# A transformer block with 32 experts on one core: the first norm's factor on columns, two weight streams alternating

## The chip, the core and the metric

The kernel runs on one core of a Trainium2 chip. The core has a matrix engine (PE, with its weight loads shown apart as PEld), a vector engine (DVE), a scalar engine (ACT), a general engine (POOL), a queue that only issues transfers (SP) and 16 DMA engines. The metric is device time in microseconds (us). All data is 32-bit float, and one product of a 128x128 block with 256 columns shows as two weight loads and two matmuls.

## What is computed

One block over 256 tokens of width 1024, batch 1. The part that the change touches is the front: a modulation row from the condition vector, an RMS norm of `x`, and the query projection; a second norm is that of the context `ctx`.

```python
def rms_norm(x, g):
    return x * lax.rsqrt(jnp.mean(x * x, axis=-1, keepdims=True) + RMS_EPS) * g

sh1, sc1, g1, sh2, sc2, g2 = silu(c) @ w_mod + b_mod        # six parts of 1024
csh1, csc1, ...            = silu(c_ctx) @ w_mod + b_mod
h  = rms_norm(x, norm1_g) * (1 + sc1) + sh1
hc = rms_norm(ctx, norm1_g) * (1 + csc1) + csh1
p  = h @ w_in            # keys, values, queries, gates
k_c, v_c = hc @ w_in[:, :512]
# global and windowed attention, gates, output projection, x = x + g1 * (...)
# second norm, router, top 4 of 32 experts, x = x + g2 * moe(...), final norm
```

## The kernel before, in words

Everything is kept transposed at the front: `x` is eight chunks of 128 features (partitions) by 256 tokens (columns), `x[:, k, :]`. So the norm's mean runs over partitions, and its factor differs from column to column.

**Streams.** All weights come on the SP queue in the order of one list, `pieces` (lines 58 to 80). A ring of eight areas, each of two halves of 1 MB, receives them; `pump` issues the next piece as soon as a half (or, for expert weights, a whole area) is free, and `done` gives a half back and calls `pump`. At the start the sixteen halves take the eight blocks `m0` (1 MB each, the modulation's shift and scale for one chunk) and the eight blocks `q` (0.5 MB each, the query weights for one chunk). The list runs `m0` 0, 1, 2, then `q` 0, `m0` 3, `q` 1 and so on: the query's blocks run two behind. `xc` (the context) is between them. ACT issues a few small transfers itself, among them a table of constants (line 296) behind the third query block.

**Norm of x (lines 205 to 218).** Each chunk is squared (five on DVE, three on ACT), and PE multiplies each square by a 128x128 matrix of ones into `ssp`, so that every partition of `ssp` has the column sums. `inv_norm` takes the square root of all 128x256 values on ACT and the reciprocal on DVE into the tile `rinv`. Then each chunk is multiplied by `rinv` (line 266, six on DVE and two on POOL).

**Modulation.** `m0_prod(j)` (line 235) multiplies the condition columns `cmod` by block `m0[j]`, in 16 small instructions; ACT copies the result to `msb`. `m0_turn(j)` (lines 243 to 248) turns it into columns on PE (`mtp`); DVE adds the bias (L244), forms the scale (L246) and modulates chunk `j` in place (L248). `crow_half` (lines 255 and 257) broadcasts `cmod` to rows `crow` on PE and ACT; the remaining modulation (`mod` blocks, on DVE and POOL, from 51 us on) needs `crow`.

**Queries.** For chunk `j`, `q_prods` adds eight products into the two PSUM tiles `qa`. The loop over `j` runs `m0_prod(j + 2)`, half of `q_prods(j)`, `m0_turn(j + 2)`, the other half. `m0` 0 and 1 and both halves of `crow` lie ahead of the loop.

**Context norm (lines 408 to 413).** During the loop ACT and POOL square and sum the context into one 128x512 tile `csq[0]`. After the second gate (`gate(1)`, line 375) PE multiplies it by ones into `csp`, `inv_norm` makes `rinv_c`, and `modulate_c` (lines 284 and 285) scales the context in place. The key projection `kp` (line 365) of `x` comes next on PE, and the context's own later.

The order on each engine is that of the program. PE takes its instructions in that order, and an instruction that waits holds back all behind it.

Of the kernel before, what the change touches and what calls it, by code (L numbers as in the profile page):

```python
# [34 lines left out]
def tile_dit_block(ctx: ExitStack, tc: tile.TileContext, xcT, consts, small, rows,  # L35
# [21 lines left out]

    for j in range(10):
        if j < 8:
            pieces.append(("m0", j, w_m0[j]))  # L60
        if j > 1:
            pieces.append(("q", j - 2, w_q[j - 2]))
        if j == 6:
            pieces.append(("xc", 0, None))
# [127 lines left out]
    th = f1.tile([128, 8, 2], F32, name="th")  # L192
    nc.scalar.activation(out=th, in_=cc, func=AF.Tanh, scale=0.5)
    nc.scalar.activation(out=junk, in_=eps, func=AF.Sqrt)
    cmod = f1.tile([128, 8, 32], F32, name="cmod")
    nc.vector.memset(cmod, 0.0)
    nc.vector.scalar_tensor_tensor(out=th, in0=th, scalar=1.0, in1=cc, op0=ALU.add, op1=ALU.mult)
    nc.vector.tensor_scalar(out=cmod[:, :, 0:2], in0=th, scalar1=0.5, scalar2=None, op0=ALU.mult)


    def t1(name):
        return f1.tile([128, 256], F32, name=name, tag="t1", bufs=5)

    ssp = ps1.tile([128, 512], F32, name="ssp", tag="y")
    for k in range(8):
        sq = t1("sq")
        v = x[:, k, :]
        if k in (0, 1, 2, 5, 7):
            nc.vector.tensor_tensor(out=sq, in0=v, in1=v, op=ALU.mult)
        else:  # L210
            nc.scalar.activation(out=sq, in_=v, func=AF.Square)
        nc.tensor.matmul(ssp[:, 0:256], ones, sq, start=(k == 0), stop=(k == 7))

    def inv_norm(ps):
        r = t1("rinv")
        nc.scalar.activation(out=r, in_=ps, func=AF.Sqrt, bias=eps, scale=1.0 / 1024)
        nc.vector.reciprocal(r, r)
        return r

# [8 lines left out]
    def m0_prod(j):  # L228


        w = take("m0", j).rearrange("p (k c) -> p k c", k=8)
        mp = ps1.tile([128, 512], F32, name="mp", tag="tp", bufs=2)
        for k in range(8):
            g = 32 * (k % 4)
            nc.tensor.matmul(mp[g:g + 32, 0:256], cmod[:, k, :], w[:, k, :], start=(k < 4), stop=(k >= 4))
        done("m0", j)
        msb_t[j] = t1("msb")
        nc.scalar.copy(out=msb_t[j], in_=mp[:, 0:256])
# [12 lines left out]
    def crow_half(h):  # L251
# [5 lines left out]
        nc.scalar.copy(out=crow[:, 512 * h:512 * h + 512], in_=cps)  # L257

    m0_prod(0)
    rinv = inv_norm(ssp[:, 0:256])  # L260
    m0_prod(1)
    crow_half(0)
    crow_half(1)
    for k in range(8):
        v = x[:, k, :]
        (nc.gpsimd if k >= 6 else nc.vector).tensor_tensor(out=v, in0=v, in1=rinv, op=ALU.mult)
        if k in (0, 2):
            m0_turn(k // 2)

# [17 lines left out]
    for j in range(8):  # L287
        if j < 6:
            m0_prod(j + 2)
        q_prods(j, range(4))  # L290
        if j < 6:
            m0_turn(j + 2)
        q_prods(j, range(4, 8))
        done("q", j)
        if j == 2:
            nc.scalar.dma_start(out=cst, in_=consts[:, C_KEEP:C_TRI])
            nc.scalar.dma_start(out=sinkb, in_=rows[0:1, 0:8].to_broadcast([128, 8]))
# [109 lines left out]
    q_chunk(3)  # L407
    csp = ps1.tile([128, 512], F32, name="csp", tag="tp", bufs=2)
    for i in range(2):
        nc.tensor.matmul(csp[:, 0:256], ones, csq[0][:, 256 * i:256 * i + 256], start=(i == 0), stop=(i == 1))  # L410
    rinv_c = inv_norm(csp[:, 0:256])
    nc.scalar.dma_start(out=tmk, in_=consts[:, C_TRI:C_END])
# [797 lines left out]
```

## Time and profile before

| | us |
|---|---|
| median of 3 runs (1194.88 to 1195.83) | 1195.11 |
| the profiled execution | 1195.13 |
| its span, first to last instruction | 1193.4 |
| PE busy in the span | 1142.9 (96%) |
| DVE, ACT, POOL busy | 359.4, 139.5, 35.7 |
| share of PE, DMA, DVE, ACT in the chain that ended last | 57%, 36%, 4%, 2% |

The chain is followed back from the last instruction: each step is what released the one after it, or the instruction ahead of it on its engine. A stretch of the chain that lies on PE with no gap says that PE was the limit there. A group in the timeline merges neighbours: its length is from its first start to its last end. The granted clock is a share of TensorE's 2.4 GHz.

### The profile page before, as it was taken

The page shows a single profiled execution, that of the slowest core. Times are in us where ns is not written, and L with a number is a line of the kernel's source. Part 1 is how long each engine was busy: PE and PEld are TensorE (multiplying, and loading weights), DVE is VectorE, ACT ScalarE, POOL GpSimd, SP SyncE. Part 2 cuts the span into 40 slices and gives each one's busy share as a digit, 9 for nine tenths or more (in the row PEclk, how much of TensorE's full clock was granted, in tenths as well). Part 3 has the DMA queues.
Part 4 walks back from the last instruction along what each step waited for, and adds up shares of the span by engine and source line. Part 5 has one row for each costly group of instructions (what it writes and reads, how often), then busy time and mean ns, then how long its engine had stood idle before and what let it go on. Part 6 is the DMA issues. An engine that isn't in the chain of part 4 may idle for free.

```text
span 1193.4 us, 13447 instructions
## 1 busy us (share of the span) xinstructions
PE 1142.9 (96%) x5722; PEld 539.0 (45%) x5722; DVE 359.4 (30%) x767; ACT 139.5 (12%) x313; POOL 35.7 (3%) x31
## 2 busy tenths in 40 slices
PE   7999999999999999999999999999898989899996
PEld 5888666884434333443434343434232424233334
DVE  3274666332122232222232222222221212121222
ACT  2122554012000000000000000000000000000012
POOL 0232000000000000000000000000000000000001
PEclk9999999999999999999999999999999999999999
DMA  9995634948999999999999999999999999999994
GB/s 378 383 387 211 225 128 153 390 177 351 427 429 426 428 426 428 429 427 428 426 429 426 429 426 428 427 428 428 428 427 427 428 428 426 429 427 429 425 428 181
DMA packets 37952, 458.34 MB, mean 384 GB/s; under 512 B 4600, under 2 KB 4992, under 8 KB 7424
## 3 DMA queue, kind: packets, MB, share of 16 engines
q1 hardware_dynamic: 36144, 454.05, 91.0%
q10 hardware_dynamic: 1744, 3.38, 0.7%
q8 instruction: 47, 0.77, 0.3%
q14 instruction: 17, 0.14, 0.0%
HBM read 456.36 MB, written 1.05 MB: 383 GB/s over the span
## 4 chain that ended last, share of the span: by engine, by line
PE 57%; DMA 36%; DVE 4%; ACT 2%; issue 1%; ACTq 0%; SPq 0%; DVEq 0%
DMA ring<-w 26%; PE u L845 20%; DMA xx<-w 10%; PE y L884 9%; PE mm L375 3%; PE xg L812 3%; PE u L695 3%; PE qa L276 2%; PE o L705 2%; PE sp L901 2%; PE br L579 2%; ACT xx L517 1%; PE yl L985 1%; PE kp L365 1%; PE vp L449 1%; DVE st L507 1%
## 5 line engine op out<-in xcount | busy, mean ns | idle before, releaser
L845 PE MATMUL u<-ring,t 128*64 128x512 f32 x1632 | 373.8, 598 | 16.1 <-DMA ring<-w 15.7
L845 PEld LDWEIGHTS u<-ring,t 128*64 128x64 f32 x1632 | 112.6, 137 | 233.3 <-issue 201.2
L884 PE MATMUL y<-ring,r_q 128*64 128x512 f32 x768 | 168.9, 592 | 0.0
L891 DVE TENSOR_TENSOR t<-y,r_kv 64x512 f32<-64x512 f32 x60 | 41.3, 689 | 325.3 <-PE y L884 324.9
L884 PEld LDWEIGHTS y<-ring,r_q 128*64 128x64 f32 x768 | 55.2, 137 | 109.6 <-issue 107.9
L858 DVE TENSOR_SCALAR r_q<-u 128x512 f32<-128x512 f32 x32 | 22.1, 692 | 248.6 <-PE u L845 248.6
L860 ACT ACTIVATE r_q<-r_q 128x512 f32<-128x512 f32 x32 | 20.1, 629 | 510.0 <-DVE r_q L858 510.0
L695 PE MATMUL u<-mtx,keep 128*64 128x512 f32 x256 | 62.2, 604 | 3.0 <-DVE r_q L861 3.0
L812 PEld LDWEIGHTS xg<-mtx,r_y 128*128 128x128 f32 x512 | 58.4, 192 | 12.2 <-issue 12.2
L812 PE MATMUL xg<-mtx,r_y 128*128 128x128 f32 x512 | 61.3, 278 | 0.0
L375 PE MATMUL mm<-xx,ring 128*128 128x256 f32 x256 | 59.9, 385 | 0.0
L901 PE MATMUL sp<-t,mtx 128*128 128x512 f32 x120 | 59.7, 620 | 0.0
L375 PEld LDWEIGHTS mm<-xx,ring 128*128 128x128 f32 x256 | 47.3, 190 | 12.6 <-issue 5.0
L845 PE MATMUL u<-xx,t 128*64 128x512 f32 x208 | 48.7, 610 | 3.7 <-DMA xx<-w 3.6
L845 PE MATMUL u<-ptt,t 128*64 128x512 f32 x208 | 48.8, 598 | 0.9 <-DMA ptt<-w 0.9
L814 DVE TENSOR_TENSOR t<-xg,modb 128x512 f32<-128x512 f32 x32 | 22.1, 692 | 86.3 <-PE xg L812 86.3
L901 PEld LDWEIGHTS sp<-t,mtx 128*128 128x128 f32 x120 | 20.5, 191 | 39.5 <-issue 39.5
L902 DVE TENSOR_TENSOR r_t<-r_t,sp 128x512 f32<-128x512 f32 x60 | 38.3, 680 | 0.0
L695 PEld LDWEIGHTS u<-mtx,keep 128*64 128x64 f32 x256 | 16.3, 135 | 44.6 <-issue 22.6
L874 ACT COPY r_q<-ta 128x512 f32<-128x512 f32 x32 | 18.8, 586 | 146.6 <-PE ta L871 146.6
L276 PE MATMUL qa<-xx,ring 128*128 128x256 f32 x128 | 30.7, 388 | 0.0
L845 PEld LDWEIGHTS u<-xx,t 128*64 128x64 f32 x208 | 14.7, 139 | 35.3 <-issue 28.1
(229 smaller groups left out, 897.4 us busy)
## 6 DMA issues: line engine op xcount, KB each, us to landing
ring<-w SPq DMA_DIRECT2D x149, 2048.0 KB, 32.4
xx<-w SPq DMA_DIRECT2D x19, 2048.0 KB, 31.0
ptt<-w SPq DMA_DIRECT2D x19, 2048.0 KB, 32.4
ring<-w_mod SPq DMA_DIRECT2D x16, 1024.0 KB, 11.2
ring<-w_in SPq DMA_DIRECT2D x10, 1024.0 KB, 9.1
ring<-w_m SPq DMA_DIRECT2D x8, 1024.0 KB, 12.6
ring<-w2l SPq DMA_DIRECT2D x3, 2048.0 KB, 34.3
ring<-w_q SPq DMA_DIRECT2D x8, 512.0 KB, 12.1
```

The source lines that it names most:

```text
L276: nc.tensor.matmul(qa[c // 4][:, c % 4, :], w[:, 128 * c:128 * c + 128], x[:, j, :], start=(j == 0 and c % 2 == 0), stop=(j == 7), skip_gr ...
L375: nc.tensor.matmul(gp[0][:, 0:256], w[:, k, :], x[:, k, :], start=(k == 0), stop=(k == 7))
L579: nc.tensor.matmul(ps[:, 0:256], w[:, k, 128 * (m % 2):128 * (m % 2) + 128], Y[:, 4 * br + k, :], start=(k == 0), stop=(k == 3))
L695: nc.tensor.matmul(u[c0:c0 + 64, ch % 2, :], ident[:, 4 * e + ch:4 * e + ch + 1].to_broadcast([128, 64]), be1, start=True, stop=False)
L705: nc.tensor.matmul(ps[:, 0:256], w[:, k, :], M[:, k, :], start=(k == 0), stop=(k == 7))
L812: nc.tensor.matmul(xp[:, b, :], z[:, tb, 128 * k:128 * k + 128], S[:, tb, :], start=(tb == 0), stop=(tb == 1))
L814: nc.vector.tensor_tensor(out=XT[p][:, 4 * h:4 * h + 4, :], in0=xp, in1=sh2[:, 4 * h:4 * h + 4].unsqueeze(2).to_broadcast([128, 4, 128]), ...
L845: nc.tensor.matmul(u[c0:c0 + 64, ch % 2, :], XT[p][:, k, 64 * j:64 * j + 64], w[:, 512 * ch:512 * ch + 512], start=False, stop=(k == 7))
L884: nc.tensor.matmul(y[64 * h:64 * h + 64, :], l, w[:, 512 * h:512 * h + 512], start=(k == 0), stop=(k == 7))
L891: nc.vector.tensor_tensor(out=YY[p][64 * j:64 * j + 64, 512 * h:512 * h + 512], in0=y[64 * h:64 * h + 64, :], in1=g2[64 * h:64 * h + 64, 5 ...
L901: nc.tensor.matmul(sp, t[:, tb, :], y[:, s], start=True, stop=True)
L902: nc.vector.tensor_tensor(out=ACC[0][:, tb, s], in0=ACC[0][:, tb, s], in1=sp, op=ALU.add)
```

## The change

It does six things. The list alternates `m0[j]`, `q[j]`, with `xc` after the sixth pair. The squares of `x` are formed two chunks at a time (two passes of 128x512 on DVE, two on ACT) and added up on DVE to one 128x512 tile `sqx[0]`. `inv_norm` takes such a tile: four products of a 128x128 piece of it with one column of ones give the sums with tokens on partitions, ACT and DVE work on 128x2 values, and two products spread the factor over rows, in PSUM. `m0_prod(0)` comes behind it. All eight products with the factor are on DVE. In the loop `m0_prod` and `m0_turn` run one ahead instead of two, and the two halves of `crow` are inside it, after `j` = 2 and 3. The context's norm uses the same `inv_norm`.

```diff
-    for j in range(10):
-        if j < 8:
-            pieces.append(("m0", j, w_m0[j]))
-        if j > 1:
-            pieces.append(("q", j - 2, w_q[j - 2]))
-        if j == 6:
+    for j in range(8):
+        pieces.append(("m0", j, w_m0[j]))
+        pieces.append(("q", j, w_q[j]))
+        if j == 5:
             pieces.append(("xc", 0, None))
...
+    for i in range(2):
+        for j in range(2):
+            v = x[:, 4 * i + 2 * j:4 * i + 2 * j + 2, :].rearrange("p a b -> p (a b)")
+            if j == 0:
+                nc.vector.tensor_tensor(out=sqx[2 * i], in0=v, in1=v, op=ALU.mult)
+            else:
+                nc.scalar.activation(out=sqx[2 * i + 1], in_=v, func=AF.Square)
+        if i == 0:
+            nc.scalar.activation(out=th, in_=cc, func=AF.Tanh, scale=0.5)
+        nc.vector.tensor_tensor(out=sqx[2 * i], in0=sqx[2 * i], in1=sqx[2 * i + 1], op=ALU.add)
+        if i == 0:
+            nc.vector.scalar_tensor_tensor(out=th, in0=th, scalar=1.0, in1=cc, op0=ALU.add, op1=ALU.mult)
+            nc.vector.tensor_scalar(out=cmod[:, :, 0:2], in0=th, scalar1=0.5, scalar2=None, op0=ALU.mult)
+    nc.scalar.activation(out=junk, in_=eps, func=AF.Sqrt)
+    nc.vector.tensor_tensor(out=sqx[0], in0=sqx[0], in1=sqx[2], op=ALU.add)
+
+    def inv_norm(sq, tag, bufs):
+
+        ps = ps1.tile([128, 512], F32, name="ssp", tag=tag, bufs=bufs)
+        for qt in range(2):
+            for i in range(2):
+                nc.tensor.matmul(ps[:, 256 + qt:257 + qt], sq[:, 256 * i + 128 * qt:256 * i + 128 * qt + 128],
+                                 ones[:, 0:1], start=(i == 0), stop=(i == 1))
+        r = f1.tile([128, 2], F32, name="rn", tag="rn", bufs=2)
+        nc.scalar.activation(out=r, in_=ps[:, 256:258], func=AF.Sqrt, bias=eps, scale=1.0 / 1024)
         nc.vector.reciprocal(r, r)
-        return r
+        for qt in range(2):
+            nc.tensor.matmul(ps[:, 128 * qt:128 * qt + 128], r[:, qt:qt + 1].to_broadcast([128, 128]), ident,
+                             start=True, stop=True)
+        return ps[:, 0:256]
...
+    rinv = inv_norm(sqx[0], "y", 1)
     m0_prod(0)
-    rinv = inv_norm(ssp[:, 0:256])
-    m0_prod(1)
-    crow_half(0)
-    crow_half(1)
     for k in range(8):
-        v = x[:, k, :]
-        (nc.gpsimd if k >= 6 else nc.vector).tensor_tensor(out=v, in0=v, in1=rinv, op=ALU.mult)
-        if k in (0, 2):
-            m0_turn(k // 2)
+        nc.vector.tensor_tensor(out=x[:, k, :], in0=x[:, k, :], in1=rinv, op=ALU.mult)
+        if k == 0:
+            m0_turn(0)
...
     for j in range(8):
-        if j < 6:
-            m0_prod(j + 2)
+        if 0 < j < 7:
+            m0_prod(j + 1)
         q_prods(j, range(4))
-        if j < 6:
-            m0_turn(j + 2)
+        if j == 0:
+            m0_prod(1)
+        elif j < 7:
+            m0_turn(j + 1)
         q_prods(j, range(4, 8))
         done("q", j)
+        if j == 0:
+            m0_turn(1)
+        if j in (2, 3):
+            crow_half(j - 2)
...
-    csp = ps1.tile([128, 512], F32, name="csp", tag="tp", bufs=2)
-    for i in range(2):
-        nc.tensor.matmul(csp[:, 0:256], ones, csq[0][:, 256 * i:256 * i + 256], start=(i == 0), stop=(i == 1))
-    rinv_c = inv_norm(csp[:, 0:256])
+    rinv_c = inv_norm(csq[0], "tp", 2)
```

## Rows read from the trace of the kernel before

**Rows 1.** Chain that ended last, 0 to 60 us: start, length, what, instructions.

```profile
6.43 5.62 PE ssp L212 x16
12.05 1.04 PE mp L235 x16
13.98 1.17 PE cps L255 x8
...
19.18 1.92 PE qa L276 x8
21.10 0.34 PE mtp L243 x4
...
46.93 8.74 PE qa L276 x40
55.67 3.45 PE mm L375 x16
```

**Rows 2.** The same chain over the whole span.

```profile
65.02 3.72 PE kp L365 x16
...
706.89 37.98 DMA xx<-w
```

**Rows 3.** Stretch of 2 us: busy by engine (instructions), granted clock, DMA share, GB/s.

```profile
276.00:278.00 2.00, 2.00 (x12) 0.65 (x10) 1.43 (x7) 0.00 (x0) 0.00 (x0) 1.00 0.01 2
```

**Rows 4.** DMA issues, 0 to 60 us: KB each, us to landing.

```profile
xx<-xcT SPq DMA_DIRECT2D x2, 512.0 KB, 4.5
```

**Rows 5.** Timeline, all engines, 0 to 60 us: start, length, engine, line, operation.

```profile
7.05 0.71 ACT L211 ACTIVATE sq<-xx 128x256 f32<-128x256 f32 x2
...
13.18 0.37 ACT L238 COPY msb<-mp 128x256 f32<-128x256 f32 x1 [4.22 <-PE mp L235]
...
17.35 0.16 DVE L244 TENSOR_TENSOR mod<-mtp,sm 128x4 f32<-128x4 f32 x1 [1.18 <-PE mtp L243]
...
17.81 0.41 DVE L248 TENSOR_SCALAR xx<-xx,a,mod 128x256 f32<-128x256 f32 x1
```

**Rows 6.** DVE by line and shape, whole span: busy us, mean ns, idle before.

```profile
L863 DVE TENSOR_TENSOR r_q<-r_q 128x512 f32<-128x512 f32 x32 | 22.1, 692 | 5.0 <-ACT r_q L860 4.9
...
L217 DVE RECIPROCAL rinv<-rinv 128x256 f32<-128x256 f32 x2 | 3.5, 1748 | 4.1 <-PE mp L235 4.1
...
L527 DVE RECIPROCAL st<-st 128x2 f32<-128x2 f32 x16 | 2.6, 164 | 7.9 <-ACT xx L517 7.7
```

**Rows 7.** ACT by line and shape, 0 to 100 us: the same columns.

```profile
L439 ACT ACTIVATE rall<-ssq,eps 128x24 f32<-128x24 f32 x1 | 0.3, 283 | 4.6 <-PE ssq L438 4.6
```

**Rows 8.** Tile `ssp`, 0 to 60 us: duration ns min/median/max, first and last start.

```profile
L212 PEld LDWEIGHTS ssp<-sq,ones x16: 190/333/338, 6.4 to 11.5; 128*128 128x128 f32 x16
```

**Rows 9.** Timeline of PE alone, 7 to 8 us: columns as in Rows 5.

```profile
7.45 1.91 PE L212 MATMUL ssp<-sq,ones 128*128 128x256 f32 x4
```

**Rows 10.** The five-microsecond stretch around it: columns as in Rows 3.

```profile
5.00:10.00 5.00, 3.57 (x8) 2.83 (x9) 2.20 (x7) 2.73 (x6) 0.00 (x0) 1.00 1.04 433
```

**Rows 11.** Timeline, all engines, 58 to 100 us: columns as in Rows 5.

```profile
58.96 0.95 PE L388 MATMUL ssq<-keep,sqq 128*128 128x2 f32 x8
...
63.44 2.35 POOL L339 TENSOR_TENSOR ring<-ring,crow 128x1024 f32<-128x1024 f32 x1 [2.61 <-DMA ring<-w_mod]
...
64.42 1.28 ACT L216 ACT_TABLE_LOAD   x1 [0.25 <-PE csp L410]
...
64.88 1.20 DVE L359 TENSOR_TENSOR sh<-sh,r_t 128x256 f32<-128x256 f32 x1
...
66.11 0.42 DVE L360 TENSOR_TENSOR r_q<-r_q,sh 128x256 f32<-128x256 f32 x1
...
85.13 1.05 PE L459 MATMUL rkp<-keep,t 128*128 128x128 f32 x8
```

**Rows 12.** Waits of the SP queue, 0 to 300 us: total, times, longest.

```profile
SPq L116 <- DMA r_t<-consts: 9.4, 1, 9.4
```

More of the change, by code (lines that the diff above doesn't have):

```diff
@@ L192, in tile_dit_block @@
     th = f1.tile([128, 8, 2], F32, name="th")
-    nc.scalar.activation(out=th, in_=cc, func=AF.Tanh, scale=0.5)
-    nc.scalar.activation(out=junk, in_=eps, func=AF.Sqrt)
     cmod = f1.tile([128, 8, 32], F32, name="cmod")
     nc.vector.memset(cmod, 0.0)
-    nc.vector.scalar_tensor_tensor(out=th, in0=th, scalar=1.0, in1=cc, op0=ALU.add, op1=ALU.mult)
-    nc.vector.tensor_scalar(out=cmod[:, :, 0:2], in0=th, scalar1=0.5, scalar2=None, op0=ALU.mult)
     def t1(name):
         return f1.tile([128, 256], F32, name=name, tag="t1", bufs=5)
-    ssp = ps1.tile([128, 512], F32, name="ssp", tag="y")
@@ L205, in tile_dit_block @@
-    for k in range(8):
-        sq = t1("sq")
-        v = x[:, k, :]
[L208 to L216, printed above, removed]
+    sqx = [tanh[i].rearrange("p a b -> p (a b)")[:, 512 * j:512 * j + 512] for i in range(2) for j in range(2)]
@@ L257, in crow_half @@
         nc.scalar.copy(out=crow[:, 512 * h:512 * h + 512], in_=cps)
+    rinv = inv_norm(sqx[0], "y", 1)
     m0_prod(0)
-    rinv = inv_norm(ssp[:, 0:256])
-    m0_prod(1)
-    crow_half(0)
-    crow_half(1)
     for k in range(8):
-        v = x[:, k, :]
-        (nc.gpsimd if k >= 6 else nc.vector).tensor_tensor(out=v, in0=v, in1=rinv, op=ALU.mult)
-        if k in (0, 2):
-            m0_turn(k // 2)
+        nc.vector.tensor_tensor(out=x[:, k, :], in0=x[:, k, :], in1=rinv, op=ALU.mult)
+        if k == 0:
+            m0_turn(0)
     qa = [ps1.tile([128, 4, 256], F32, name="qa", tag="s", bufs=2) for _ in range(2)]
```

## The prediction

> **What bounds the kernel now.** I read the chain of waits first. In its first 55 us it lies on PE almost without a gap: the column sums from 6.43, the first two modulation products from 12.05, the two halves of `crow` from 13.98, the first query half-block at 19.18, then 36.49 us to 55.67, where the gates begin [rows 1]. So PE sets the pace at the front; the reader is to see that each row begins about where the one before it ended. The chain of the whole span goes on through PE, with short stretches on DVE and ACT in the attention, and turns to the weight transfers only at 706.89 [rows 2]. Does a shift at 55 us reach the end? The windows view says yes: at 276 to 278 us the DMA engines are idle (share 0.01, 2 GB/s) [rows 3]. All ten weight areas are then full, since the list's first ten expert pieces take the ring's eight areas and the two that are added after attention, and the next transfer waits for PE to give one back. The stream that ends the kernel therefore starts when PE gets there, so a shift on PE before 276 goes to the end one for one. The other order of the list pairs the pieces in other halves of the ring, but by the code the same ten are placed before the experts start.
>
> The sum is made against the profiled execution, 1195.13 us, a span of 1193.4 and 1.73 around it; the median of the runs, 1195.11, is the same to 0.02.
>
> **Part 1, up to the first modulation product.** Removed from PE: the 16 instructions on the squares, 5.62 us, 6.43 to 12.05 [rows 1]. In their place stands a chain over four engines. The first half of `x` lands 4.5 us after its issue at 0.76, at 5.3 [rows 4]. For the second half there is no row; ACT's second square reads it and starts by 7.4 (half of the 0.71 us pair from 7.05 on) [rows 5], and DVE in the new order comes to it at 7.0, so it adds 0 to 0.4. DVE now makes five passes of 128x512 in a row: square, add, two tiny ones for `cmod`, square, add, add. A pass of that shape takes 0.69 [rows 6] and the tiny ones I take at 0.16 like L244 [rows 5]: 5.3 + 5 x 0.69 + 2 x 0.16 = 9.1. ACT's squares lie beside it. Then PE does eight loads and eight matmuls of one column; the same form with two columns took 0.95 for eight [rows 11]. That was at full speed. At the start PE is slower: the weight loads of `ssp` took 333 ns at the median against 190 at the least [rows 8], a factor of 1.75, and four 128x256 matmuls took 1.91 us [rows 9] where eight of the query took 1.92 [rows 1]. The granted clock of that stretch prints 1.00 [rows 10], but I read half speed, the lower of TensorE's two levels (1.2 and 2.4 GHz). So 0.95 x 1.75 = 1.7, to 10.8. ACT's root 0.28 at most [rows 7], DVE's reciprocal of 128x2 0.16 instead of 1.75 [rows 6], three handoffs of some 0.05, then two spreading products: half of the eight instructions that took 1.05 [rows 11], times 1.75, 0.9. Together **12.4** for the start of `m0_prod(0)`, against 12.05 before. The PE work that is taken out was not ahead of idle time: the new chain is as long.
>
> **Part 2, to the first query block.** Before, one modulation product took half of 1.04 x 2, 1.04 alone in the chain for 16 instructions [rows 1]; at the lower level 1.8. Then ACT's copy 0.37 with handoffs 0.1 [rows 5], `m0_turn` 0.34 on PE [rows 1] (0.6), and DVE from the start of L244 to the end of L248, 17.35 to 18.22, 0.9 with its handoff [rows 5]. Now nothing lies between these steps for PE, while before it had a second product and `crow` there. First query matmul: 12.4 + 1.04 + 0.47 + 0.34 + 0.9 = 15.2 at the upper level, 16.2 at the lower. Before: 19.18. The seven further products of `x` with the factor, 0.42 each on DVE, lie beside the 5 us of query block 0; the two that POOL had cost nothing there.
>
> **Part 3, the loop.** Earlier by 3 to 4 us, but with more left to do: one more modulation product (1.04), one more turn (0.34), two halves of `crow` (1.17 each) [rows 1], 3.7 together. 36.49 + 3.7 = 40.2, so the queries end at 55.4 or 56.4 against 55.67: -0.3 to +0.7. Where the lower level lasts into the first query half-block, that takes 3.8 instead of 1.92 and adds up to 1.9; I take 0.9, half of it, since before the rise came within the unbroken run of the column sums (16 in 5.62 us is some seven at 0.48 and nine at 0.24) [rows 1, 9], and here the work before `q_prods(0)` has gaps. That is **+1.6** (bounds -0.3 and +3.0, with 0.4 for the second half of `x`). The alternating stream itself gives nothing: the query's first block could be used at 16 at the earliest, and by the 433 GB/s of the stretch [rows 10] a pair of 1.5 MB takes 3.6 us while PE needs 5.2 for it (two half-blocks, a product and a turn), so blocks stay ahead of PE in either order.
>
> **Part 4, the context's norm.** This is the part that I think decides. Before, PE left the sums `csp` and went on to `kp` at 65.02, released by DVE's reading of the query tile [rows 2]; the root and the 1.75 us reciprocal lay on ACT and DVE beside it. Now PE itself needs the factor back, for two spreading products ahead of `kp`, and every later matmul queues behind them. The factor is late: ACT must load the table for the root, 64.42 to 65.70, then 0.28; DVE must finish `q_chunk(3)`, whose last step ends at 66.53 [rows 11]; then 0.16 for the reciprocal [rows 6], 0.1 of handoffs, and half of 1.05 for the products, some 0.45 until `kp` can follow [rows 11]. 66.53 + 0.16 + 0.1 + 0.45 = 67.2: **2.2 us** later than 65.02. The step L359 took 1.20 us here while POOL ran a product until 65.79, where other steps take 0.42 [rows 11]; if POOL's product falls elsewhere the table load decides, 65.70 + 0.28 + 0.16 + 0.1 + 0.45 = 66.7, and 66.4 if the load starts without waiting for PE: 1.4 at the least. I take **2.1**, bounds 1.4 and 2.4. PE has no gap later in which this could be recovered before 76 us, and DVE's 1.6 us saved is not on the chain there.
>
> Sum: 1.6 + 2.1 = 3.7, **1198.8 us**, with bounds 1196.2 and 1200.5.
>
> **The clock as a rival.** Before the change PE ran at the lower level through the eight column-sum products, which cost little more than they had to wait for anyway, and was at the upper one for all useful products [rows 1, 9]. If the broken work at the new start keeps it at the lower level through the whole first query block, sixteen instructions cost 3.8 us more: 0.7 + 3.8 + 2.1 = 6.6, **1201.7**. It decides from the point where the rise comes after 18 us. For it speaks that PE is idle until 9.1 and has three gaps of half a microsecond or more until 16; against it, that the rise came quickly before. The Trainium skill, "TensorE: Matmul & The Clock Gate", Part 1, says that the throttled state is the default and that sustained activity releases it; by that rule a beginning of small products separated by waits is the wrong one, and the time would be this rival's. The trace of before agrees as far as it goes: 333 ns a load at first, 190 later.
>
> **Waits covered, no change.** The upper level from 12.4 on and the shortest handoffs: 0 at the front and 1.6 for the context, **1196.7**. For it: the bounds reach there. It needs both at their low ends.
>
> **Not slower.** PE is a bound at the front, and the change takes 5.6 us of it out. If the DVE and PE parts of the factor are shorter than the rows say, so that `m0_prod(0)` starts at 9.0, when its block can just have landed (1.6 MB behind the first half of `x`, 3.7 us after 5.3) [rows 10], all that follows comes 3.4 earlier, -3.7 at the upper level; with 1.4 for the context, -2.3: **1192.8**, at the edge of what counts as faster. It decides where the sum tile stands at 6.5 instead of 9.1. Against it: five passes at 0.69 cannot fit between 5.3 and 6.5.
>
> **The stream stops.** Before, SP once waited 9.4 us for ACT's table of constants to land, holding back a query block [rows 12]. ACT issues it behind the third block; in the new order `crow` stands ahead of it, so it goes out at about 33 (16.2 + 3 x 5.2 + 1.2), and what is held back can be a modulation block. If that is `m0` 4, wanted at 32 (16.2 + 3 x 5.2) and held until 42 by as long a wait, the loss is 10 us: **1209**. If it is block 6 or later, wanted from 42 on, it costs nothing; I think so, since more pieces are out by then.
>
> **How the numbers follow.** Forecast 0.56, clock 0.12, covered 0.14, not slower 0.12, stream 0.06. The range takes the forecast, the covered case and the clock, 1196.0 to 1201.8, and leaves out 0.18. A measurement of this kernel can tell about 0.2% from no change, 2.4 us. Slower: 0.56 + 0.12 + 0.06 = 0.74. The covered case and half of the not-slower one are within it: 0.20; the other half is faster: 0.06.
>
> **What would show it.** In the changed trace the first modulation product starts near 12.4, the first query matmul between 15 and 17, the gates at 56 to 58.5 (part 1 to 3); weight loads of 333 ns up to or beyond 16 show the clock. At the context's norm PE should stand idle some 2 us, released by DVE's reciprocal, before the two spreading products and `kp` (part 4), and `kp` should start near 69 in absolute time. From there to the experts all should be as before, later by one constant, and the DMA idle at some 280. Wrong would be: PE idle on a ring block, `m0_prod(0)` before 11, or `kp` following the norm without a gap.

## The result, and the profile after

The changed kernel takes **1203.3 us** (median of 5 runs, 1200.18 to 1204.55) where the kernel before takes 1195.39 beside it (5 runs, 1194.88 to 1197.96): a ratio of 1.0057, 95% interval 1.0040 to 1.0074. It is slower by 7.9 us, twice the 3.7 that the sum gave. The profiled execution took 1203.51, its span is 1201.7, so 8.3 more than the span before. Of 84 runs of the kernel before beside this and the later kernels (three more, of 1490 us and longer, left out), 22 lie near 1198 and the others near 1195.5, so 2 us between two single executions need not be the kernels'.

The chain of waits of the changed kernel, 8 to 62 us (start, length, what, instructions), which answers [rows 1]:

```profile
9.31 1.88 PE ssp L219 x8
...
11.73 1.22 PE ssp L225 x4
12.96 1.91 PE mp L244 x16
...
15.31 1.03 PE mtp L252 x4
...
17.29 3.62 PE qa L281 x8
20.91 1.00 PE mp L244 x16
21.91 1.92 PE qa L281 x8
23.84 0.34 PE mtp L252 x4
24.18 1.00 PE mp L244 x16
...
34.41 0.89 PE cps L264 x8
...
54.75 5.29 PE qa L281 x24
60.04 3.45 PE mm L386 x16
```

Three things are to be seen. The first query half-block begins 1.89 earlier than before (17.29 against 19.18), yet the gates begin 4.37 later (60.04 against 55.67). All of PE's work until 20.9 runs at half speed, TensorE's lower level of 1.2 GHz: a modulation product takes 1.91, then 1.00; a turn 1.03, then 0.34 (on PE's own timeline 1.01 and 0.50, since the chain leaves out what overlaps its neighbours); the first half-block 3.62, the next 1.92. And between the first half-block and the gates lie seven modulation products, where the chain before had five left.

PE's busy time in stretches of five microseconds (columns as in [rows 3]), changed kernel:

```profile
5.00:10.00 5.00, 0.69 (x4) 0.69 (x4) 3.62 (x7) 2.85 (x5) 0.00 (x0) 1.00 1.04 427
10.00:15.00 5.00, 4.27 (x26) 2.62 (x26) 0.59 (x2) 0.37 (x2) 0.00 (x0) 1.00 1.02 424
15.00:20.00 5.00, 3.72 (x10) 3.11 (x11) 3.12 (x10) 0.26 (x1) 0.00 (x0) 1.00 1.00 411
...
70.00:75.00 5.00, 4.64 (x16) 3.92 (x17) 4.17 (x14) 3.41 (x9) 2.37 (x1) 0.68 1.00 411
...
284.00:286.00 2.00, 2.00 (x12) 0.60 (x10) 1.91 (x9) 0.00 (x0) 0.00 (x0) 1.00 0.02 8
```

The DMA engines' idle stretch lies at 284 to 286, eight later than in [rows 3]: a shift on PE went through to the end, as forecast. In 70 to 75 the granted clock is 0.68. The chain there:

```profile
68.55 0.13 ACT L222
...
69.85 0.27 ACT rn L222
...
70.14 0.18 DVE rn L223
...
70.36 0.71 PE ssp L225 x4
71.07 5.14 PE kp L376 x16
```

and on PE's timeline, with the idle time before it and what ended it:

```profile
70.36 0.71 PE L225 MATMUL ssp<-keep,rn 128*128 128x128 f32 x4 [1.74 <-DVE rn L223]
```

This is the context's norm. The key projection starts 11.03 behind the gates' begin (71.07 - 60.04), before 9.35 (65.02 - 55.67) [rows 1, 2]: +1.68. Then its first sixteen instructions take 5.14 instead of 3.72 [rows 2], because the clock fell (0.68 in that stretch), just behind PE's 1.74 us without work: +1.42. One more step lies far behind, in the chain at 217 us:

```profile
217.43 1.75 PE y L562 x16
...
219.61 0.44 DVE r_y L567
...
220.09 6.09 PE br L587 x27
```

PE waits here for DVE to have read the last attention tile before it can start on the branch projection `br`; before, `br` followed at 211.69 without a gap. That is +0.93.

The books close: 4.37 + 1.68 + 1.42 + 0.93 = 8.40, and `br` starts 8.40 later (220.09 - 211.69). From there to the end nothing is added.

### The profile page after: what moved, and what is told of

It reads as the page before. It is cut to its first block, busy times and chain, and to the rows that moved or that the text cites. A ratio compares the mean times of both kernels' runs of the same rounds, so it can differ in the third digit from the quotient of the medians.

```text
span 1201.7 us, 13440 instructions
## 1 busy us (share of the span) xinstructions
PE 1142.8 (95%) x5726; PEld 540.8 (45%) x5726; DVE 356.8 (30%) x769; ACT 139.3 (12%) x312; POOL 33.9 (3%) x29
## 4 chain that ended last, share of the span: by engine, by line
PE 56%; DMA 36%; DVE 4%; ACT 2%; issue 1%; ACTq 0%; SPq 0%; DVEq 0%
DMA ring<-w 26%; PE u L853 20%; DMA ptt<-w 10%; PE y L892 9%; PE mm L386 3%; PE xg L820 3%; PE u L703 3%; PE qa L281 3%; PE o L713 2%; PE sp L909 2%; PE br L587 2%; PE kp L376 1%; ACT xx L525 1%; PE yl L993 1%; PE vp L457 1%; DVE st L515 1%
## 5 line engine op out<-in xcount | busy, mean ns | idle before, releaser
L386 PEld LDWEIGHTS mm<-xx,ring 128*128 128x128 f32 x256 | 47.3, 190 | 12.6 <-issue 5.0
L853 PEld LDWEIGHTS u<-ptt,t 128*64 128x64 f32 x208 | 14.5, 137 | 34.9 <-issue 27.6
## 6 DMA issues: line engine op xcount, KB each, us to landing
ring<-w_q SPq DMA_DIRECT2D x8, 512.0 KB, 12.6
```

The lines of the kernel that those rows point to most:

```text
L386: nc.tensor.matmul(gp[0][:, 0:256], w[:, k, :], x[:, k, :], start=(k == 0), stop=(k == 7))
L853: nc.tensor.matmul(u[c0:c0 + 64, ch % 2, :], XT[p][:, k, 64 * j:64 * j + 64], w[:, 512 * ch:512 * ch + 512], start=False, stop=(k == 7))
```

## The experiments

Each kernel had runs of the kernel before beside it (medians between 1195.53 and 1196.16), and the ratio is to those. Times in us. "Query" is the start of the first query product, "gates" the end of the queries, "kp" the key projection's distance behind it, all from the profiled execution's chain (for a3_warm the last two from PE's timeline, in which the changed kernel has 59.87 and 11.04). Unless a diff says otherwise, a's start from the changed kernel and b's and d's from the kernel before.

| | median | ratio to before, 95% | query | gates | kp |
|---|---|---|---|---|---|
| before | 1195.39 | | 19.18 | 55.67 | 9.35 |
| changed | 1203.3 | 1.0057 [1.0040, 1.0074] | 17.29 | 60.04 | 11.03 |
| b2_stream | 1196.06 | 1.0002 [0.9993, 1.0012] | 19.51 | 56.00 | 9.35 |
| b3_norm_x | 1197.95 | 1.0013 [1.0004, 1.0023] | 20.84 | 57.33 | 9.34 |
| b5_loop | 1199.24 | 1.0024 [1.0014, 1.0034] | 16.75 | 59.45 | 9.35 |
| b4_warm | 1194.51 | 0.9989 [0.9979, 0.9998] | 18.40 | 54.89 | 9.34 |
| a3_warm | 1201.56 | 1.0050 [1.0033, 1.0067] | 14.79 | 57.38 | 11.04 |
| a5_all_fill | 1199.53 | 1.0022 [1.0012, 1.0032] | 16.07 | 58.51 | 11.03 |
| a6_pool | 1197.86 | 1.0015 [1.0005, 1.0025] | 15.89 | 56.75 | 11.19 |
| a2_ctx_rows | 1200.42 | 1.0048 [1.0031, 1.0064] | 16.94 | 59.24 | 9.34 |
| a4_fill | 1201.70 | 1.0057 [1.0040, 1.0074] | 16.72 | 57.84 | 11.03 |
| b1_ctx_cols | 1199.82 | 1.0028 [1.0017, 1.0039] | 20.17 | 56.66 | 12.35 |
| a1_bank | 1202.06 | 1.0054 [1.0037, 1.0071] | 17.15 | 59.65 | 11.03 |
| d1_busy | 1191.99 | 0.9967 [0.9955, 0.9980] | 15.72 | 52.26 | 9.34 |
| d4_cold | 1194.34 | 0.9981 [0.9971, 0.9992] | 21.40 | 59.88 | 9.34 |
| d3_order | 1192.48 | 0.9966 [0.9954, 0.9979] | 13.36 | 52.69 | 9.35 |
| d2_early_q | 1192.26 | 0.9966 [0.9954, 0.9979] | 14.53 | 52.29 | 9.34 |

The theory after the result: the front's loss is the lower clock that a broken beginning brings, plus work that the new loop leaves for later; the rest is the context's norm, a clock fall behind it, and a PSUM bank. The rivals: the list's order, the column norm as such, or POOL.

### One part of the change at a time

**b2_stream**: the alternating list alone.

```diff
-    for j in range(10): ...            # q two behind m0
+    for j in range(8):
+        pieces.append(("m0", j, w_m0[j]))
+        pieces.append(("q", j, w_q[j]))
```

> The kernel before with one part of the change alone: the list of weight pieces alternates m0 and q blocks; norms, loop and context as before. My theory (the stream is not a limit in either order): the queries end at 55.5 +- 0.3 us as before, key projection 9.5 us behind the gates' begin, time within 1 us of the kernel before, 1194.5 to 1196.5. Rival: in the order before, modulation blocks are used two ahead; with the alternating list m0 block j+2 lies one query block later in the queue, so PE waits for it: at least one PE wait of 1 us or more on a ring block in the loop and a time 1 to 3 us longer.

Gates at 56.00, 0.33 later; the time is the same. The list's order is neither the loss nor a gain.

**b3_norm_x**: the norm of `x` on columns alone, with the old list, loop and context norm.

```diff
+    rinv = inv_norm(sqx[0], "y", 1)        # sums, root, reciprocal on columns; rows copied by ACT
     m0_prod(0)
-    rinv = inv_norm(ssp[:, 0:256])
     m0_prod(1)
     crow_half(0)
```

> The kernel before with the norm of x alone taken on columns (ACT copies the spread factor to SBUF, so that crow finds its bank free); stream, loop and context as before. Theory (the column sums warmed PE; small products with waits do not): the first modulation product starts near 12.9 instead of 12.0, it, the second one and crow run at the lower clock, and the queries end 2.5 to 4 us later. Rival (the loss at the front is in the loop, where products and crow were moved): within 1 us of the kernel before.

The queries end 1.66 later. The chain, 9 to 21 us:

```profile
9.15 1.88 PE ssp L221 x8
...
11.57 1.22 PE ssp L227 x4
12.79 2.92 PE mp L247 x32
15.71 1.10 PE cps L267 x8
```

Two products take 2.92 where two at full speed take 2.0. So taking 5.6 us of column sums off PE made PE later, by two things: the first product begins 0.74 later, since the new chain is longer than the sums were (12.79 against 12.05 [rows 1]), and 0.92 comes from the two slow products. The sums that went were done while PE came to full speed, and now the useful products pay for that.

**b5_loop**: list and loop as in the change, norms on rows as before.

```diff
     rinv = inv_norm(ssp[:, 0:256])
+    m0_prod(0)
-    m0_prod(1)
-    crow_half(0)
-    crow_half(1)
...                                       # loop one ahead, crow after j = 2, 3, as in the change
```

> The kernel before with the order of the stream and of the loop alone changed: blocks alternate, products and turns run one ahead, crow is inside the loop; both norms on rows. Theory: the first query product starts near 15.8 instead of 19.1, PE stands some 1.6 us before it, and 4.1 us of work are left over for the loop: the queries end 1 to 1.5 us later, up to 1.7 more if the clock falls in that gap and 1.2 more where POOL's product holds DVE in the last turn. Rival (the loop is the front's loss): 3 us or more in every execution.

The queries end 3.78 later. In this execution PE waited 2.1 us for the first modulated chunk (DVE's 1.76 us reciprocal lies ahead of it), and the clock fell behind that wait: the first half-block took 2.70 and the next product 1.87, together 1.65 above full speed. So it mixes clock (1.65) and order with its wait (the other 2.13). Its ten runs, 1198.66 to 1200.16, are 2.5 us or more above the median beside them; d3_order has the order at full speed.

### Is it the clock?

**b4_warm**: the kernel before with idle products (ones by ones, result not read) while PE waits for `x`.

```diff
+    warm = ps1.tile([128, 512], F32, name="warm", tag="y")
+    for i in range(12):
+        nc.tensor.matmul(warm[:, 0:128], ones, ones, start=True, stop=True)
```

> The kernel before with 12 idle products (ones by ones, result not read) ahead of the column sums of x, nothing else. What it tells apart: whether the lower clock at the front costs anything in the kernel before. Theory (the eight column sums cost what PE takes for them, 5.62 us from 6.43, more than half of it at the lower level): with the upper level from the start the sums end near 10.3 to 11 instead of 12.05, the queries end 1 to 1.8 us earlier than 55.5, time 1193.5 to 1194.5. Rival (the squares from DVE and ACT, or the m0 block, set the pace, or the idle products do not bring the upper level in time): sums end at 11.5 to 12.1 and the time is within 0.5 us of the kernel before.

Tile `ssp` (columns as in [rows 8]):

```profile
L215 PEld LDWEIGHTS ssp<-sq,ones x16: 187/190/190, 6.9 to 10.0; 128*128 128x128 f32 x16
```

The loads took 190 ns at the median where they took 333 [rows 8], and the last one began 1.5 us earlier. Of these 0.78 reach the gates, less than the 1 at least that was expected, since the second modulation block is then what PE waits for (its transfer ends the chain until 12.16). The time is 1.25 lower.

**a3_warm**: the changed kernel with 28 idle products at the start.

```diff
+    warm = ps1.tile([128, 512], F32, name="warm", tag="mm")
+    for i in range(28):
+        nc.tensor.matmul(warm[:, 0:128], ones, ones, start=True, stop=True)
```

> The changed kernel with 28 idle products of ones by ones (128x128) on PE from about 1 to 9 us, before the column sums of x; their result is not read. Theory (clock): at the front the lower level costs 0.9 in the sums, 0.5 in the spreading, 0.9 in the first modulation product, 0.6 in its turn and 1.7 in the first query half-block, 4.6 us together; with PE at its upper level from 9 us on, the first query product starts near 14.5 instead of 17.3 and the queries end near 55.5 instead of 60.0: 4.5 us less than the changed kernel. Rival (order and handoffs): the steps between the engines stay, and no more than 1.5 us are won.

The sums took 0.80 instead of 1.88, the first product 1.04 instead of 1.91, and the queries began 2.5 earlier. But then the clock fell again, behind the gaps of the turn's chain. Chain and stretch of that execution:

```profile
14.79 2.90 PE qa L284 x8
17.70 1.72 PE mp L247 x16
```

```profile
16.00:18.00 2.00, 2.00 (x8) 1.00 (x11) 1.06 (x4) 0.00 (x0) 0.00 (x0) 0.50 1.09 438
```

The gates come 2.5 earlier (57.38 against 59.87 by the same view), not the 4.5 expected. So in this execution a warm start was not enough where PE stood in three gaps behind it.

**a5_all_fill**: idle products at the start, in those gaps and at the context's norm, and the bank as in a1_bank.

```diff
+    for i in range(28): ...               # start
+        for i in range(3): ...            # behind the norm's sums
+            for i in range(3): ...        # ahead of the first turn
+            for i in range(5): ...        # behind it
+            for i in range(7): ...        # at the context's norm
```

> The changed kernel with idle products of ones by ones wherever PE stood or began slow: 28 ahead of the first sums, 3, 3 and 5 in the three waits before the first query block, 7 in the context's wait, and the PSUM tags in the old order. Their results are not read; every step of the change stays. Theory (of the front's 4.4 us nearly all is the lower clock, and the 1.4 behind the context's norm too): the queries end at 55.5 to 56.2 instead of 60.0, kp to vp takes 16.5, no gap before br, and what is left over the kernel before is the context's wait, 1.7 us, and up to 0.7: about 1197.5. Rival (the front's order itself costs): the queries end near 58 and about 1200 is left.

Full speed throughout the front, and the gates still begin at 58.51: the theory's 55.5 to 56.2 fell. The timeline shows why (start, length, engine, line; in brackets the wait and what ended it):

```profile
51.89 2.40 DVE L264 TENSOR_SCALAR a<-mod,sm 128x2 f32<-128x2 f32 x1
51.92 2.34 POOL L365 TENSOR_TENSOR ring<-ring,crow 128x1024 f32<-128x1024 f32 x1 [3.40 <-PE mtp L261]
...
54.79 2.42 PE L296 MATMUL qa<-xx,ring 128*128 128x256 f32 x10 [1.30 <-DVE xx L266]
```

A step on two columns that takes 0.23 elsewhere takes 2.40 while POOL runs one product, and PE waits 1.30 for it. The Trainium skill, "SBUF — State Buffer", section "SBUF: two separate sides", says that the vector engine and GpSimd share a port pair which one of them holds for a whole instruction while the other is blocked; for the vector engine it names instructions in a two-port mode, or with two SBUF inputs against a GpSimd one that reads SBUF. The row agrees that one blocks the other, DVE's step ending 0.03 behind POOL's; which of those two conditions it meets no run shows. Before, PE's part of the last turn ended at 46.9, ahead of POOL's first product on the ring (51.02); the loop that runs one ahead moves it into POOL's time. In the changed kernel's own profiled execution the last turn just missed it.

**a6_pool**: a5_all_fill with POOL's products held back by a copy that needs the query tile.

```diff
     q_chunk(0)
+    hold = f1.tile([128, 1], F32, name="hold")
+    nc.gpsimd.tensor_copy(hold, Q[:, 0, 0:1])
```

> The changed kernel with idle products in every gap of PE at the front and at the context's norm (results not read), as in the run a5_all_fill, and POOL's first products of the remaining modulation held back until a part of the query tile is written, so that POOL does not work while DVE forms the last modulated chunk. Theory (DVE's two-column step for the last chunk took 2.4 us there because POOL ran a product beside it, and PE waited 1.3 us for it): the step takes under 0.6 us, PE's wait before the eighth query block is under 0.2 us, the queries end near 57.0 instead of 58.35. Rival (the wait is the turn's own chain, PE to DVE and back): the wait stays over 1 us and the queries end at 58.0 to 58.6. In either case the held products come later, and the time may not gain.

```profile
51.70 0.23 DVE L264 TENSOR_SCALAR a<-mod,sm 128x2 f32<-128x2 f32 x1
```

The step takes 0.23, PE does not wait, the gates begin at 56.75. So with full speed and without POOL the changed front is still 1.08 behind the kernel before, and the 3.29 from here to the changed kernel's 60.04 goes with the lower clock at its beginning: 1.40 at the first query product (17.29 - 15.89) and 1.88 in the first half-block (3.62 against 1.74). The 1.08 is not the order alone. The idle products stand in PE's chain themselves: without those in the gaps, a3_warm reached its first query product at 14.79, 1.10 earlier. An estimate from these two runs puts a full-speed front without idle products in the gaps at 55.65 (56.75 - 1.10), level with the kernel before; no run shows that front.

### The context's norm and the bank

**a2_ctx_rows**: the changed kernel with the context's norm on rows again.

```diff
-    rinv_c = inv_norm(csq[0], "tp", 2)
+    csp = ps1.tile([128, 512], F32, name="csp", tag="tp", bufs=2)
+    for i in range(2):
+        nc.tensor.matmul(csp[:, 0:256], ones, csq[0][:, 256 * i:256 * i + 256], start=(i == 0), stop=(i == 1))
+    rinv_c = t1("rinv")                    # root and reciprocal on 128x256
```

> The changed kernel with the context's norm taken on rows again, as in the kernel before; the front stays changed. Theory (wait and clock): PE loses 1.7 us in the wait for the factor and 1.4 us more because the clock falls behind it; both go, kp takes 3.7 us instead of 5.1, and the time is 3.1 us less than the changed kernel, about 5 us over the kernel before. Rival (wait alone; the fall of the clock is due to something else): 1.7 us less, kp still 5.1. Rival from the prediction (the front costs 1.6): only 2 us over the kernel before are left.

`kp` is 9.34 behind the gates again and takes 3.72: wait and clock fall are both gone (3.1 together), and the time is 2.9 under the changed kernel's. (The fronts of single executions differ too; see a4_fill.)

**b1_ctx_cols**: the other way round, the context's norm on columns put into the kernel before.

```diff
-    csp = ps1.tile([128, 512], F32, name="csp", tag="tp", bufs=2)
-    for i in range(2):
-        nc.tensor.matmul(csp[:, 0:256], ones, csq[0][:, 256 * i:256 * i + 256], start=(i == 0), stop=(i == 1))
-    rinv_c = inv_norm(csp[:, 0:256])
+    rinv_c = inv_norm_cols(csq[0], "tp", 2)    # the change's inv_norm
```

> The kernel before with the context's norm alone taken on columns. Theory: kp starts 11.0 us behind the end of the queries instead of 9.4, a wait of 1.7 us that nothing gives back, and in some executions 1.4 us more where the clock falls behind it: 1.7 to 3.1 us over the kernel before. Rival (the wait comes from the shifted front, where POOL's products fall on the query's rotation): kp stays within 0.5 us of 9.4 and the time is the same.

```profile
65.95 1.26 DVE sh L375
...
67.78 1.23 PE ssp L232 x4
69.01 5.79 PE kp L381 x16
```

`kp` is 3.0 farther behind the gates: the 1.7, DVE's step at 65.95, which takes 0.4 otherwise, and spreading products that take 1.23 instead of 0.71; and the clock fell here too, `kp` taking 5.79. PE's wait is 2.54 here, and the spreading products, at 1.23, already ran slow. The median is 3.7 above the one beside it, more than the 1.7 to 3.1 expected. (Its front is that of the kernel before and yet ends 0.99 later in this execution.)

**a4_fill**: seven idle products between the context's sums and the spreading products.

```diff
+            fill = ps1.tile([128, 512], F32, name="fill", tag="mm")
+            for i in range(7):
+                nc.tensor.matmul(fill[:, 0:128], ones, ones, start=True, stop=True)
```

> The changed kernel with seven idle products of ones by ones on PE between the context's column sums and the spreading of its factor; their result is not read. The wait for the factor stays. Theory (the clock falls because PE stands still there): kp takes 3.7 us instead of 5.1 and the time is 1.4 us less than the changed kernel. Rival (the fall has another cause, or comes with the one-column products): kp stays at 5.1 and the time is the same. In neither does kp start earlier than 11.0 us behind the end of the queries.

The distance stays 11.03, `kp` takes 3.46, no fall. But a3_warm had the same 1.74 us wait without filler and no fall either. Of four profiled executions with that wait unfilled (2.54 in b1_ctx_cols, 1.74 in the others) three show the fall (changed, a1_bank, b1_ctx_cols), and of three with it filled none: it fits that the wait brings the fall, and that it does so in some executions only. More the runs do not settle.

The front of this kernel is the changed one, instruction for instruction, and yet its gates begin at 57.84:

```profile
16.72 1.99 PE qa L285 x8
57.84 3.45 PE mm L390 x16
```

The first half-block ran at full speed here, 1.63 shorter, and began 0.57 earlier (0.41 from a faster turn, 0.16 since the sums began earlier): 2.20 together, the whole distance to 60.04. Behind the same front the first half-block took 3.62 (changed), 3.37 (a1_bank), 1.99 (a2_ctx_rows) and 1.99 (a4_fill). So the front's loss is not one number: 4.37 in the changed kernel's profiled execution, 2.17 in this one.

**a1_bank**: `mtp` allocated behind the norm's tile, as the kernel before has it.

```diff
-    mtp = ps1.tile([128, 8, 2, 2], F32, name="mtp", tag="mm")
...
     rinv = inv_norm(sqx[0], "y", 1)
+    mtp = ps1.tile([128, 8, 2, 2], F32, name="mtp", tag="mm")
```

> The changed kernel, with one line moved: the PSUM tile mtp is created behind the norm's tile ssp, so that the tags get their banks in the order of the kernel before. Theory: the 0.9 us that PE stands before the first output product br (219.2 to 220.1, released by DVE's last r_y) come from br falling on a bank that the last attention tile y still holds; then br follows y without a gap and the time is 0.9 us less than the changed kernel, about 7 us over the kernel before. Rival: the gap comes from attention running later against DVE and ACT; then it stays at 0.9 us and the time does not move.

```profile
217.05 1.73 PE y L562 x16
218.78 7.32 PE br L587 x33
```

The gap ahead of `br` is gone. PE's timeline has it, 0.93 each time, in the four kernels in which `mtp` is created ahead of the norm's tile (changed, a2_ctx_rows, a3_warm, a4_fill) and in none of the other thirteen. That in the change two tags changed banks, so that the second pool's tile for `br` fell on the bank of the attention's last tile, is read from the code; no view shows the banks. The diff's line that does it is one that looks like nothing: a definition that now stands ahead of another.

### What the column norm is worth when PE has other work

**d1_busy**: the old list, loop and context norm; the norm of `x` on columns, but 16 idle products first, then `crow`'s products ahead of the sums and a modulation product between sums and spreading.

```diff
+    for i in range(16):
+        nc.tensor.matmul(warm[:, 0:128], ones, ones, start=True, stop=True)
...
+    for b in range(8):                     # crow's products, into a tile of their own
+        nc.tensor.matmul(cps[:, b // 4, 128 * (b % 4):128 * (b % 4) + 128], ...)
...
+    norm_sums()
     m0_prod(0)
+    norm_rows()
     m0_prod(1)
```

> A version that keeps the kernel before's stream, loop and context norm on rows, and takes the norm of x on columns with PE kept in work from the first us: 16 idle products (result not read), then the crow products, then the four sum products, the first modulation product, then the two spreading products, the second modulation product. Theory (the columns are worth what they take off PE if PE has other work of the kernel beside the chain over ACT and DVE, and if the upper level holds): PE has the upper level from about 7 us, the first query product comes at 15.5 to 17.5 instead of 19.1, the queries end at 52 to 54, time 1192 to 1194. Rival (the handoffs DVE to PE to ACT to DVE to PE and the supply of blocks hold the front as long as the sums did): queries end at 55 or later, time 1195 or more.

Chain and stretches:

```profile
3.37 12.21 DMA ring<-w_q
...
15.72 1.97 PE qa L288 x8
...
52.26 3.45 PE mm L387 x16
```

```profile
5.00:10.00 5.00, 4.26 (x37) 3.94 (x36) 3.62 (x7) 2.85 (x5) 0.00 (x0) 1.00 1.04 431
10.00:15.00 5.00, 4.60 (x59) 3.11 (x62) 1.91 (x7) 1.92 (x4) 0.00 (x0) 1.00 1.01 423
```

The queries end 3.41 earlier than before and the time is 3.8 lower, 1191.99 (1191.82 to 1192.31): **faster than both kernels**. The same chain over DVE and ACT stands here; PE works beside it instead of standing. At the first query product it is now the block's transfer that ends last. The 3.41 is not the column norm's alone: idle products gave 0.78 at the gates by themselves (b4_warm), and `crow` moved forward. No run gives the norm on rows the same beginning, so how much of the 3.41 is the column norm's is not shown.

**d4_cold**: d1_busy with 1 idle product instead of 16, nothing else.

```diff
-    for i in range(16):
-        nc.tensor.matmul(warm[:, 0:128], ones, ones, start=True, stop=True)
+    nc.tensor.matmul(warm[:, 0:128], ones, ones, start=True, stop=True)
```

> d1_busy with 1 idle product instead of 16, so that PE begins with the crow products at 7.1 us. Theory (the idle products are worth the lower clock that they take away): the crow products, the sums and the first modulation products run at the lower level, 16 loads of 333 ns instead of 110, the first modulation product comes at 11.5 to 12.5 instead of 10.2, the first query product at 17 to 18.5 and the queries end at 53.5 to 55.5, time 1193.3 to 1195.5. Rival (the chain over DVE and ACT and the landing of the query's block at 15.6 hide it): first query product at 15.6 to 16.4, queries end at 52 to 52.8, time within 0.8 us of d1_busy's 1192.0.

```profile
7.12 3.75 PE cps L223 x16
10.87 1.50 PE ssp L231 x8
12.37 1.86 PE mp L255 x16
...
21.40 3.71 PE qa L287 x8
...
51.14 8.74 PE qa L287 x40
59.88 3.45 PE mm L386 x16
```

The same order, and the gates begin 7.62 later than in d1_busy, beyond the theory's 55.5: half speed up to 25 us. This execution took 1200.18, the longest of the ten of this kernel, which go down to 1192.60, while d1_busy's six lie within 0.5. Only this one of the ten is profiled, so that the other nine differ by the moment of full speed is likely and not shown; here its price is 7.62. By the medians it is 2.35 (1194.34 against 1191.99), as expected, and even without the idle products this kernel is 0.19% faster than the kernel before. The Trainium skill, "TensorE: Matmul & The Clock Gate", Part 1, says that the number of slow products at a start varies from run to run; the four first half-blocks behind one front (a4_fill) agree. It also says that the start's penalty is under 1% of a typical span; here it is up to 0.6%, which is all that the change was about.

**d3_order**: the change's list and loop behind d1_busy's front, `crow` staying in the front.

```diff
-    m0_prod(1)
     for k in range(8):
...
-        if k in (0, 2):
-            m0_turn(k // 2)
+        if k == 0:
+            m0_turn(0)
...                                       # list and loop as in the change, without crow_half
```

> d1_busy's front (idle products, then the crow products, sums, first modulation product, spreading products) with the change's list (alternating) and the change's loop (modulation product and turn one ahead, the second product inside the loop). The crow halves stay in the front, the context's norm is on rows. Theory (the change's order alone costs what it leaves for later minus what it starts earlier: two products of 1.0 and a turn of 0.34 more, 2.4 in all with the broken blocks, first query product at 14.0 to 14.7): queries end at 52.6 to 53.6, 0.5 to 1.5 later than d1_busy, time 1192.5 to 1193.5, faster than the kernel before. Rival (the order one ahead has its own waits, the turn's chain from PE over ACT and DVE back, over 1 us in all, or POOL's products again lengthen the last turn): queries end at 54.5 or later, time 1194.5 or more.

```profile
13.36 1.99 PE qa L285 x8
...
52.69 3.45 PE mm L388 x16
```

First product 2.36 earlier than in d1_busy, gates 0.43 later, the time within 0.5. Without `crow` in it, the order one ahead is neutral once full speed holds: what starts earlier pays for what is left over (two products, a turn, broken blocks).

**d2_early_q**: d1_busy with each query block one behind its modulation block instead of two, and half of the query ahead of the loop's product.

```diff
+        q_prods(j, range(4))
         if j < 6:
             m0_prod(j + 2)
-        q_prods(j, range(4))
-        if j < 6:
-            m0_turn(j + 2)
         q_prods(j, range(4, 8))
+        if j < 6:
+            m0_turn(j + 2)
```

> d1_busy with the query's blocks one behind the modulation's in the list instead of two, and the loop's product and turn for chunk j + 2 each half a query block later; all else as there. In d1_busy the first query product waits for its block, which lands at 15.6 us, while the modulated chunk is ready at 14.5. Theory (the list's order is worth what the first query block's landing costs, once PE's front is early): first query product at 14.4 to 14.7 instead of 15.7, queries end near 50.9 instead of 52.1, time 1190.6 to 1191.3. Rival (what is moved forward is paid for behind it, the third modulation block landing later than PE wants it): queries end at 51.7 to 52.5, time within 0.5 us of d1_busy's 1192.0.

First product at 14.53 as the theory had it, gates at 52.29 as the rival had it, the same as d1_busy: the product that used to fill the wait for the block now comes behind it. An earlier first query product is no gain in itself where PE had other work in that place.

## Why the prediction was wrong in size

The direction and the place (front and context norm) held, and the forecast +3.7 became +8.4 in the profiled execution. By the prediction's steps:

- **What bounds the kernel**: right. PE at the front, and every shift went to the end one for one (8.40 at `br`, 8.3 in the span).
- **Part 1**, `m0_prod(0)` at 12.4: it began at 12.96. The sums began at 9.31 (9.1 foreseen), took 1.88 (1.7), the spreading 1.22 (0.9), all at the lower level that the step had read from the 333 ns loads. Its terms as listed add up to 12.3, not 12.4. Right but for 0.56; "as long as before" held.
- **Part 2**, first query product at 15.2 or 16.2: 17.29. Product and turn ran at half speed throughout. The sum went on with the later value (its 0.7 comes from 16.2), and 17.29 is 1.09 later still: 0.56 from part 1, and 0.43 from the turn, which took 1.03. The 0.6 for it was scaled from a 0.34 in which the chain leaves out what overlaps; standing alone before, at full speed, a turn took 0.61.
- **Part 3, the step that failed**, +1.6 (at most 3.0) where +4.37 came. 1.09 is the late begin from part 2; two terms are its own. First the left-over, which the step put at one more modulation product, one more turn and two halves of `crow`, 3.7. Behind the first query product the old chain had five products left and the new has seven, so two: `m0_prod(2)` had stood ahead of 19.18 in the old order. Two products 2.0, a turn 0.34, the halves 0.89 each at full speed instead of 1.17, and 0.4 for half-blocks now broken by products: 4.5. Second the clock: 0.9 was taken for the first half-block, it cost 1.70 there (3.62 - 1.92). -1.89 + 4.5 + 1.70 is 4.3 of the 4.37. a4_fill separates them behind the same front: with the half-block at full speed 4.6 were left over (57.84 - 16.72 - 36.49) and the step came to +2.17, inside its bounds; the other 2.20 is the clock, but for 0.16.
- **The alternating stream gives nothing**: right (b2_stream, d2_early_q).
- **Part 4**, +2.1, bounds 1.4 and 2.4: 1.68. POOL's product had ended earlier here (67.2), and ACT's table load decided, 68.55 to 69.83, with the root behind it until 70.11; DVE's last query step ended at the same time. The step had worked that case out at 1.7.
- **Not in the sum at all**: the clock's fall behind that wait, 1.42 (this execution, not each), and the bank, 0.93 (a1_bank).
- **The rivals.** The clock: its condition, full speed only after 18 us, came true (20.9), and it cost 1.70 of the 3.8 in the half-block and, against a6_pool, 1.40 ahead of it. It was given 0.12; of the four profiled executions with this front two had the half-block slow (changed, a1_bank), so 0.12 looks low. Waits covered, and not slower: false. The stream stops: SP waited 12.6 us for ACT's table, and PE waited for no block.

What the prediction argued for an early return of full speed, that it came quickly within the old column sums, was evidence for an unbroken run only; its own sentence said so and the number did not follow it.

## What to carry to other kernels

Before taking work off the engine that is the limit, ask what fills the place, and at which clock the rest will run: the same column norm cost 1.7 us where PE then stood (b3_norm_x), and with `crow` and idle products in the place the stage ended 3.4 earlier (d1_busy). Where a start's clock differs from execution to execution, do not put one price on it from one trace. When a loop's look-ahead changes, count what is left on the bound engine from one common instruction to the end of the stage, in both orders, instead of listing what was moved. And a changed order of first allocations is part of a diff: look at which tiles later share a bank.

## What the runs showed of the hardware that was not expected

- Full speed can come late although PE is almost unbroken: in d4_cold's profiled execution PE was busy 5.00 of 10 to 15 us and 4.65 of 15 to 20, and the half-block from 21.40 on still ran at half speed. In the seven kernels that begin with 12 or more idle products the sums ran at full speed each time.
- The granted-clock column prints 1.00 for 10 to 20 us of the changed kernel, where every duration is that of half speed. At a kernel's start the durations are to be read, not the column.
- A two-column step on DVE took 2.0 to 2.4 us beside one POOL product (0.23 without), in a2_ctx_rows and a5_all_fill; a5's row has it as long as that product itself.
